# Layer 1's modulation vectors: from TensorE matmuls to multiply-accumulate on VectorE

## The chip, the cores and the metric

One core of a Trainium2 chip runs the whole program. The metric is the device time of one execution in microseconds (us), the median of several runs. A profiled execution gives the trace from which the rows below are taken. TensorE is PE in the profile (PEld are its weight loads), VectorE is DVE, ScalarE ACT, GpSimd POOL, and SP is the engine whose queue issues all loads.

## The reference

Two layers run over 256 context tokens and 256 latent tokens of 1024 channels, in fp32. At the head of each layer stand six modulation vectors per stream (shift, scale and gate for the mixer, and the same for the channel part):

```
sc, scc = silu(c), silu(c_ctx)                  # 1024 values each
mod_x = split(sc  @ mod_w[i] + mod_b[i], 6)     # mod_w[i]: 1024 x 6144
mod_c = split(scc @ mod_w[i] + mod_b[i], 6)
h  = rmsnorm(x) * (1 + scale) + shift;  x = x + gate * mixer(h)
h2 = rmsnorm(x) * (1 + scale2) + shift2;  x = x + gate2 * ffn(h2)
```

The context stream does the same with `mod_c`. Layer 0 has a dense feed-forward part (SwiGLU with 2816 hidden channels), layer 1 a top-2-of-8 mixture of experts. In the last layer the context is needed only for the recurrence's final state, so of `mod_c` only the first two vectors are used there. The modulation vectors depend on `c` and `c_ctx` alone, so layer 1's can be made at any time before its first norm.

## The kernel before

Tokens lie along the free dimension (context 0 to 255, latent 256 to 511), channels along the partitions in 8 tiles of 128. A projection goes *piece* by piece: a piece is 128 output channels x 1024 inputs of weights (128x1024 fp32, 512 KB). Each piece is split into a high and a low half by `split`/`hilo` (L160 on ACT makes `wh`, L161 on DVE makes `wl`; three buffers of each), and `mm` (L245 to L247) runs 8 x 3 matmuls of 512 columns for it (high x high, high x low, low x high) into one PSUM bank, then calls `tick`. DVE takes the pieces as they come; splits are put ahead in the order of issue by a priority.

The weights of the dense part come in chunks of four pieces (2 MB) into the `raw` ring of two buffers, all through SP's queue, in the order of the list `PLAN`, which `_stream_plan` writes at build time. `hold` hands out the pieces and fetches the next chunk when the last one is used up. A chunk `("mod", i, q)` in that list is not handed out: it starts `mod_chunk(i, q)`, which runs as a background generator stepped by `tick`.

`mod_chunk` makes four blocks of 128 modulation values for both streams from one 2 MB chunk. The weights are the moving operand: 8 matmuls (L341) of 512 columns, their stationary operand 32 columns wide, in four column groups of the array, add up in the PSUM tile `pmod`. For layer 1 four chunks share one bank; then ACT copies it to `ev` (L346), four small matmuls against `sel` add up the partial sums into `pmt` (L351), and one DVE addition (L365) puts them with the bias into `mod[1]`, a 128x48x2 tile (block, stream). Layer 1's twelve chunks stand in `PLAN` behind the first four chunks of layer 0's branch projections, and behind the chunks of `MOD_AFTER` in its feed-forward part.

`ffn` works in groups of 256 hidden channels, `NG` = 11. The first two groups run stream by stream on two held chunks. Then for each g from 2 to 10 `up(g)` runs four full-width pieces (two of w1, two of w3; Silu on ACT, product at L700 and its low half on DVE), and `down(g-2)` projects two pieces back: 8 x 2 x 3 matmuls (L719 to L721) and 16 residual updates on DVE (L554). At the end the last three groups are projected stream by stream, with layer 1's first norm (which reads `mod[1]`) as background work in between. Hidden tiles are four `ya` buffers a group, of sixteen; the tags `g` (16 buffers) and `cv` (8) are tiles of 128x512 which the mixer uses otherwise.

Everything is scheduled at build time: the order in time of each engine is a fixed list in which work that is not ready yields to work that is, and semaphores make each instruction wait for its data and buffers.

Of the kernel before, what the change touches and what calls it, by code (L numbers as in the profile page):

```python
# [6 lines left out]
F32 = mybir.dt.float32  # L7
F32R = mybir.dt.float32r
I32 = mybir.dt.int32
AF = mybir.ActivationFunctionType  # L10
# [75 lines left out]
def _chunks(p):  # L86
    return [p[q:q + 4] for q in range(0, len(p), 4)]
# [25 lines left out]
def _stream_plan():  # L113
    plan = [("lru", 0, 0), ("lru", 1, 0)]
    for n, c in enumerate(_chunks(_win_order(0))):
        if n == 0:
            plan += [("mod", 0, 0), tuple(c)] + [("mod", 0, q) for q in range(1, 4)]
        else:
            plan.append(tuple(c))
        if 2 <= n < 10:  # L120
            plan.append(("mod", 0, n + 2))
    for n, c in enumerate(_chunks(_branch_order(0))):
        plan.append(tuple(c))
        if n < 4:
            plan.append(("mod", 1, n))
    q = 4
    for n, c in enumerate(_chunks(_ffn_order() + _win_order(1) + _branch_order(1))):
        plan.append(tuple(c))
        if n in MOD_AFTER:
            plan.append(("mod", 1, q))  # L130
            q += 1
    assert q == 12, q
    return plan


NG = NF // 2
MOD_AFTER = (3, 5, 6, 8, 9, 11, 12, 14)
PLAN = _stream_plan()


class Trunk:
    def __init__(self, ctx, tc, wd, wm, xt, vec, out, dbg=None, stop=None):
        self.tc, self.nc = tc, tc.nc
        self.wd, self.wm, self.xt_d, self.vec_d, self.out = wd, wm, xt, vec, out
        self.dbg, self.stop = dbg or {}, stop
        self.ci = DEPTH
        self.ahead = 100
        self.last_act = None
        self.gate = None
        self.moddue = False  # L150
        self.pend = []
        self.bgs = []
        self.run(ctx)

    def v(self, key, i=0, n=1):
# [44 lines left out]
    def tick(self):  # L200
        for g in list(self.bgs):
            self.step(g)
        self.start_mod()

    def drain(self):
        while self.bgs:
            self.tick()

    def split(self, src):
        hi = self.hl.tile([P, PIECE], F32R, tag="wh", name="wh")  # L210
# [529 lines left out]
    def ffn(self, X, h, nxt):  # L740
        upn = lambda g: [self.hold((w, 0, 2 * g + f)) for w in ("w1", "w3") for f in range(2)]
        dnn = lambda g: [self.hold(("w2", 0, 2 * g + f)) for f in range(2)]
        hid = {}

        def new(g):
            hid[g] = [(self.t2("ya", "hh", F32R), self.t2("ya", "hl", F32R)) for f in range(2)]
            return hid[g]

        r0, r1 = upn(0), upn(1)
        new(0)  # L750
        new(1)
        for s in range(2):
            for g, r in ((0, r0), (1, r1)):
                self.up(r, h, s * TC, (s + 1) * TC, hid[g])
            if s == 0:
                self.drain()
        for g in range(2, NG):
            u = upn(g)
            self.up(u, h, 0, T, new(g))
            if g < NG - 1:  # L760
                self.down(dnn(g - 2), hid.pop(g - 2), X)
        self.drain()
        self.preload(AF.Sqrt)
        last = range(NG - 3, NG)
        r = [dnn(g) for g in last]
        for s in range(2):
            self.down_last(r, [hid[g] for g in last], s, X)
            nxt(s)
        self.dump("xf0", X)
# [11 lines left out]
    def run(self, ctx):  # L781
        tc, nc = self.tc, self.nc
        self.cst = ctx.enter_context(tc.tile_pool(name="cst", bufs=1))
        self.vec = self.cst.tile([P, NV], F32, tag="vec", name="vec")
        xs = self.cst.tile([P, KD, TC], F32, tag="xs", name="xs")
        self.small = ctx.enter_context(tc.tile_pool(name="small", bufs=2))
        self.mod = [self.cst.tile([P, 48, 2], F32, tag=f"mod{i}", name=f"mod{i}") for i in range(DEPTH)]
        self.sc = self.cst.tile([P, KD, SCW], F32, tag="sc", name="sc")
        nc.sync.dma_start(self.vec[:, 0:NV0], self.vec_d[:, 0:NV0])
        nc.sync.dma_start(self.sc, self.vec_d[:, NV:NV + KD * SCW].rearrange("p (k m) -> p k m", m=SCW))  # L790
        self.act_f(self.sc, self.sc, AF.Silu)
        W = dict(reuse_waits="tile")
        tags = {"ya": 16, "g": 16, "cv": 8, "hx": 16, "lt": 2}
        left, right, base = ExitStack(), ExitStack(), ExitStack()
        xc = left.enter_context(tc.tile_pool(name="xc", bufs=1)).tile([P, KD, TC], F32, tag="xc", name="xc")
        X = [(xc[:, k, :], xs[:, k, :]) for k in range(KD)]
        self.psum = base.enter_context(tc.tile_pool(name="psum", bufs=8, space=bass.MemoryType.PSUM))
        self.hl = left.enter_context(tc.tile_pool(name="hl", bufs=3))
        self.raw = left.enter_context(tc.tile_pool(name="raw", bufs=2))
        actr = right.enter_context(tc.tile_pool(name="actr", bufs=1, side="right"))  # L800
        self.lrup = right.enter_context(tc.tile_pool(name="lrup", bufs=2, side="right"))
        self.t2 = lambda tag, name, dt=F32: (actl if tag == "ya" else actr).tile(
            [P, 512], dt, tag=tag, name=name, bufs=tags[tag])
        start = tc.tile_pool(name="start", bufs=2)
        self.start = start.__enter__()
        m0 = self.chunk(("mod", 0, 0), self.start)
        for k in range(0, KD, 2):
            for s, t in enumerate((xc, xs)):
                nc.sync.dma_start(t[:, k:k + 2, :], self.xt_d[s, :, k:k + 2, :])
        hx = self.pairs("hx")  # L810
        self.lru_begin(0)
        u = self.begin(X, hx, m0)
        self.lru_consts()
        start.__exit__(None, None, None)
        actl = left.enter_context(tc.tile_pool(name="actl", bufs=1, **W))
        m = self.mixer(0, X, hx, u)
        self.preload(AF.Sqrt)
        h2 = self.pairs("hx")
        gs2 = self.gains(0, "n2", 4)

        def norm2(s, j):
            if j == 7:
                self.bgs.append(self.norm_steps(0, X, s * TC, (s + 1) * TC, gs2, 3, h2))

        self.mix_out(0, X, m, (0, 1), norm2)
        if self.stop == "m0":
            self.drain()
            left.close(), right.close(), base.close()
            return
        hx1 = []  # L830

        def norm1(s):
            if s == 0:
                hx1.extend(self.pairs("hx"))
            self.bgs.append(self.norm_steps(1, X, s * TC, (s + 1) * TC, self.gains(1, "n1", 1), 0, hx1, LAG1[s]))

        self.ffn(X, h2, norm1)
        self.lru_begin(1)
        m = self.mixer(1, X, hx1)
        self.preload(AF.Sqrt)  # L840
        right.close()
        self.mrawa = ctx.enter_context(tc.tile_pool(name="mrawa", bufs=RINGA, side="right", **W))
        self.rp = ctx.enter_context(tc.tile_pool(name="rp", bufs=1, side="right", **W))
        self.ptok = None
        self.bgs.append(self.route_begin())
        self.tick()
        self.mi, self.mq = 0, []

        def route(s, j):
            if j < 3:  # L850
                for _ in range(RINGA // 3):
                    self.mfetch()
            if j:
                self.route_tile(X, j - 1)

        self.mix_out(1, X, m, (1,), route)
        self.route_tile(X, KD - 1)
        assert self.ci == len(PLAN) and not self.bgs
        left.close()
        if self.stop == "m1":  # L860
            base.close()
            return
        self.mtok = ctx.enter_context(tc.tile_pool(name="mtok", bufs=1, **W))
        self.mrawb = ctx.enter_context(tc.tile_pool(name="mrawb", bufs=RINGB, **W))
        self.hl = ctx.enter_context(tc.tile_pool(name="mhl", bufs=3, **W))
        self.mp = ctx.enter_context(tc.tile_pool(name="mp", bufs=1, **W))
        self.moe(X)
        base.close()
# [452 lines left out]
def layout(inputs):  # L1321
# [51 lines left out]
    for n, what in enumerate(PLAN):  # L1373
        if what[0] == "mod":
            _, i, q = what
            w = a["mod_w"][i].reshape(KD, P, 48, P)
            cols = [2 * q, 2 * q + 1, KD + 2 * q, KD + 2 * q + 1] if i == 0 and q < 4 else range(4 * q, 4 * q + 4)
            d = wd[n].reshape(P, KD, 4, P)
# [21 lines left out]
        wm[:, :, 0:2].reshape(NE, NMC, 2, P, KD // 2, 2, 256)[:, :, :, :, :, g] = w  # L1400
    wm[:, :, 2] = a["moe_w2"][0].reshape(NE, NMC, 2, P, D).transpose(0, 1, 3, 2, 4).reshape(NE, NMC, P, MCH)
    wm = wm.reshape(NE * NJ, P, MCH)
    return {"wd": wd, "wm": wm, "xt": np.ascontiguousarray(xt), "vec": vec}


# [17 lines left out]
```

## Time and profile before

| | |
|---|---|
| median of 3 runs | 1915.62 us (1915.62 to 1917.23) |
| the profiled execution | 1915.24 us, span 1913.5 us |
| mean granted TensorE clock | 0.988 |
| busy, share of the span | PE 97%, PEld 74%, DVE 64%, ACT 47%, POOL 0% |
| HBM read | 445.73 MB |

The span runs from the first to the last instruction; what is outside it is start and end of the program. Busy time is the time in which at least one instruction of an engine is under way. Matmuls are pipelined, so the time between the starts of two of them says more than their durations.

### The profile page before, as it was taken

To read this page: it belongs to the slowest core of one execution; us is meant where nothing else is said; L and a number is where in the kernel's file an instruction comes from. 1 tells how busy PE (TensorE), PEld (TensorE's weight loads), DVE (VectorE), ACT (ScalarE), POOL (GpSimd) and SP (SyncE) were. 2 spreads that over 40 slices of the span, in tenths; PEclk is the share of its full clock that TensorE was granted. 3 is DMA by queue.
4 is the path that set the end of the run, shared out by engine and by line. 5 is a ranking of instruction groups with operands and counts; after the bars stand their busy time and mean duration, and the time that the engine had idled before them with its cause. 6 is when DMAs were issued, how large, how long until landed. Compare 5 with 4: busy or idle time off the path is not lost. (4 is left out here: it accounts for less than half of the span.)

```text
span 1913.5 us, 26733 instructions
## 1 busy us (share of the span) xinstructions
PE 1853.5 (97%) x10508; PEld 1420.8 (74%) x10508; DVE 1215.8 (64%) x1995; ACT 893.5 (47%) x1265; POOL 0.2 (0%) x4
## 2 busy tenths in 40 slices
PE   6999999999999999999999999899999999999997
PEld 3667777777997777779778899687578658767853
DVE  3899995355664544545899665786289249618932
ACT  4685322343552122134689464674167137416711
POOL 0000000000000000000000000000000000000000
PEclk8999999999999999999999999799999999999999
DMA  9234444244233244241233447689999999999994
GB/s 350 99 109 144 170 176 176 88 153 156 89 111 144 104 188 159 101 191 60 100 110 133 176 177 286 253 339 364 419 419 417 388 419 419 389 411 419 417 394 162
DMA packets 54277, 448.59 MB, mean 234 GB/s; under 512 B 6016, under 2 KB 7168, under 8 KB 10496
## 3 DMA queue, kind: packets, MB, share of 16 engines
q1 hardware_dynamic: 54144, 446.80, 59.8%
q8 instruction: 85, 1.39, 0.3%
q14 instruction: 48, 0.39, 0.1%
HBM read 445.73 MB, written 1.05 MB: 233 GB/s over the span
## 5 line engine op out<-in xcount | busy, mean ns | idle before, releaser
L160 ACT ACTIVATE wh<-raw 128x1024 fp32r<-128x1024 f32 (+1 forms) x237 | 246.9, 1053 | 455.1 <-PE ps L246 256.3
L161 DVE TENSOR_TENSOR wl<-raw,wh 128x1024 fp32r<-128x1024 f32 (+1 forms) x237 | 285.9, 1216 | 179.7 <-ACT wh L160 177.1
L161 DVE TENSOR_TENSOR wl<-mraw,wh 128x1024 fp32r<-128x1024 f32 x264 | 314.5, 1222 | 35.7 <-ACT wh L160 29.2
L160 ACT ACTIVATE wh<-mraw 128x1024 fp32r<-128x1024 f32 x264 | 272.8, 1058 | 51.5 <-PE s L1159 37.8
L245 PE MATMUL ps<-nh,wh 128*128 128x512 f32 (+1 forms) x736 | 274.1, 372 | 1.8 <-ACT wh L160 1.8
L247 PE MATMUL ps<-nh,wl 128*128 128x512 f32 (+1 forms) x736 | 269.5, 366 | 3.1 <-DVE wl L161 3.1
L246 PE MATMUL ps<-nl,wh 128*128 128x512 f32 (+1 forms) x736 | 269.3, 366 | 0.0
L245 PEld LDWEIGHTS ps<-nh,wh 128*128 128x128 f32 x736 | 139.5, 190 | 38.4 <-issue 4.7
L1170 PE MATMUL s<-mraw,xes 128*64 128x256 f32 x1408 | 162.0, 380 | 0.0
L247 PEld LDWEIGHTS ps<-nh,wl 128*128 128x128 f32 x736 | 139.5, 190 | 27.9 <-DVE wl L161 3.3
L246 PEld LDWEIGHTS ps<-nl,wh 128*128 128x128 f32 x736 | 139.5, 190 | 25.0 <-issue 1.4
L1160 PE MATMUL s<-wl,xe 128*128 128x512 f32 x352 | 140.5, 399 | 4.2 <-DVE wl L161 4.2
L1158 PE MATMUL s<-wh,xe 128*128 128x512 f32 x352 | 143.0, 406 | 0.0
L228 ACT ACTIVATE hd<-s 128x256 f32<-128x256 f32 (+1 forms) x88 | 28.9, 328 | 242.6 <-PE s L1170 218.6
L1159 PE MATMUL s<-wh,xe 128*128 128x512 f32 x352 | 139.0, 395 | 0.0
L1170 PEld LDWEIGHTS s<-mraw,xes 128*64 128x64 f32 x1408 | 98.4, 137 | 44.8 <-issue 0.7
L1179 DVE TENSOR_TENSOR hd<-hd,s 128x256 f32<-128x256 f32 (+1 forms) x88 | 30.9, 351 | 129.8 <-ACT hd L228 129.8
L544 DVE SCALAR_TENSOR_TENSOR cv<-v,vec,cv 128x254 f32<-128x254 f32 (+14 forms) x240 | 102.5, 469 | 0.8
L1160 PEld LDWEIGHTS s<-wl,xe 128*128 128x128 f32 x352 | 66.9, 190 | 23.0 <-DVE wl L161 8.9
L1225 PE MATMUL y<-mraw,hs 128*64 128x512 f32 x352 | 83.4, 595 | 0.4 <-DVE hs L1204 0.4
L1158 PEld LDWEIGHTS s<-wh,xe 128*128 128x128 f32 x352 | 67.3, 191 | 13.4 <-ACT wh L160 0.6
L1159 PEld LDWEIGHTS s<-wh,xe 128*128 128x128 f32 x352 | 67.2, 191 | 12.7
(278 smaller groups left out, 3474.0 us busy)
## 6 DMA issues: line engine op xcount, KB each, us to landing
mraw<-in_wm_dram SPq DMA_DIRECT2D x264, 1024.0 KB, 9.4
raw<-in_wd_dram SPq DMA_DIRECT2D x77, 2048.0 KB, 7.8
lw<-in_wd_dram SPq DMA_DIRECT2D x16, 256.0 KB, 2.7
xc<-in_xt_dram SPq DMA_DIRECT2D x4, 256.0 KB, 10.9
xs<-in_xt_dram SPq DMA_DIRECT2D x4, 256.0 KB, 10.8
out_dram<-xs SPq DMA_DIRECT2D x8, 128.0 KB, 2.0
vec<-in_vec_dram SPq DMA_DIRECT2D x1, 636.0 KB, 15.4
vec<-in_vec_dram SPq DMA_DIRECT2D x1, 317.0 KB, 2.9
```

The costliest lines, as they stand in the source:

```text
L160: return (self.nc.scalar.activation(hi, src, AF.Copy), self.nc.vector.tensor_tensor(lo, src, hi.bitcast(F32), op=ALU.subtract))
L161: self.nc.vector.tensor_tensor(lo, src, hi.bitcast(F32), op=ALU.subtract))
L245: self.nc.tensor.matmul(o, wh, ah, start=(k == 0), stop=False)
L246: self.nc.tensor.matmul(o, wh, al, start=False, stop=False)
L247: self.nc.tensor.matmul(o, wl, ah, start=False, stop=(k == KD - 1))
L544: nc.vector.scalar_tensor_tensor(cv[:, a0:a1], v[:, a0 + d:a1 + d], w(t), cv[:, a0:a1], op0=ALU.mult, op1=ALU.add)
L1158: nc.tensor.matmul(p1, xe[0][:, k, :], wh[:, cs], start=(k == 0), stop=False)
L1159: nc.tensor.matmul(p1, xe[1][:, k, :], wh[:, cs], start=False, stop=False)
L1160: nc.tensor.matmul(p1, xe[0][:, k, :], wl[:, cs], start=False, stop=(k == KD - 1))
L1170: nc.tensor.matmul(p1[r, 0:2 * P].rearrange("p (g f) -> p g f", g=2), xe[:, k, :], w[:, :, h * P:(h + 1) * P], start=(k == 0), stop=(k == ...
L1179: self.nc.vector.tensor_tensor(hd, hd, p1[:, n:2 * n], op=ALU.mult)
L1225: ins = self.nc.tensor.matmul(py[0][r, :], hs[:, f * HALF:(f + 1) * HALF], raw[:, f * PIECE + q * 512:f * PIECE + (q + 1) * 512], start=(c ...
```

## The change

Layer 1's twelve `mod` chunks leave `PLAN`. In their place a generator `mod_rows` runs in `ffn` from g = 2 on, one step with each `tick`, and `down` is followed by a `tick` more. That is six steps to a group. It loads `silu`'s arguments, `c` and `c_ctx`, each laid out as a row on all 128 partitions (`sr`, four tiles of 128x512 in `ya` buffers), and applies Silu on ACT. Then for each of the 48 blocks it has the weights with the 128 output channels on the partitions and the 1024 inputs along the free dimension (`wv`, two tiles of 128x512 in `cv` buffers, loaded two steps ahead). One DVE instruction per half multiplies the weights by the row and keeps the sum over its 512 columns (`accum_out`); blocks 0 to 15 do so for both streams, blocks 16 to 47 for the latent stream alone. A small instruction adds the two halves and the bias into `mod[1]`, which a memset on GpSimd has set to zero at the start. The products themselves go to a `g` tile that nobody reads.

```diff
@@ _stream_plan @@
         plan.append(tuple(c))
-        if n < 4:
-            plan.append(("mod", 1, n))
-    q = 4
-    for n, c in enumerate(_chunks(_ffn_order() + _win_order(1) + _branch_order(1))):
-        plan.append(tuple(c))
-        if n in MOD_AFTER:
-            plan.append(("mod", 1, q))
-            q += 1
-    assert q == 12, q
+    plan += [tuple(c) for c in _chunks(_ffn_order() + _win_order(1) + _branch_order(1))]
     return plan
...
@@ tick, drain @@
         self.start_mod()
+        if self.slow and next(self.slow, None) is None:
+            self.slow = None
 
     def drain(self):
+        slow, self.slow = self.slow, None
         while self.bgs:
             self.tick()
+        self.slow = slow
+
+    def mod_rows(self):
+        nc = self.nc
+        nb = 6 * KD
+        rows = [self.t2("ya", "scr") for _ in range(4)]
+        for q, t in enumerate(rows):
+            nc.sync.dma_start(t, self.sr[:, q * 512:(q + 1) * 512])
+            self.act_f(t, t, AF.Silu)
+        raw = {}
+
+        def fetch(b):
+            raw[b] = [self.t2("cv", "wv") for _ in range(2)]
+            for h, t in enumerate(raw[b]):
+                nc.sync.dma_start(t, self.wv[b, :, h * 512:(h + 1) * 512])
+
+        fetch(0)
+        fetch(1)
+        for b in range(nb):
+            yield 1
+            if b + 2 < nb:
+                fetch(b + 2)
+            n = 2 if b < 2 * KD else 1
+            acc = self.small.tile([P, 2, 2], F32, tag="acc", name="acc")
+            w = raw.pop(b)
+            junk = self.t2("g", "junk")
+            for s in range(n):
+                for h in range(2):
+                    nc.vector.scalar_tensor_tensor(junk, w[h], 1.0, rows[2 * s + h], op0=ALU.mult, op1=ALU.mult,
+                                                   accum_out=acc[:, h, s:s + 1])
+            nc.vector.scalar_tensor_tensor(self.mod[1][:, b, 0:n], acc[:, 0, 0:n], self.v(("mb", 1), b), acc[:, 1, 0:n],
+                                           op0=ALU.add, op1=ALU.add)
...
@@ ffn @@
+        self.slow = self.mod_rows()
         for g in range(2, NG):
             u = upn(g)
             self.up(u, h, 0, T, new(g))
             if g < NG - 1:
                 self.down(dnn(g - 2), hid.pop(g - 2), X)
+                self.tick()
+        while self.slow:
+            self.tick()
         self.drain()
...
@@ run @@
+        nc.gpsimd.memset(self.mod[1], 0.0)
...
@@ layout @@
+    wv = np.ascontiguousarray(a["mod_w"][1].T.reshape(6 * KD, P, D))
+    sr = np.tile(np.concatenate([a["c"][0], a["c_ctx"]])[None], (P, 1)).astype(f32)
```

## Rows read from the trace of the kernel before

**Rows 1.** The page's busy times: us, share of the span, number of instructions.

```profile
PE 1853.5 (97%) x10508; PEld 1420.8 (74%) x10508; DVE 1215.8 (64%) x1995; ACT 893.5 (47%) x1265; POOL 0.2 (0%) x4
```

**Rows 2.** Busy time by stage, as its header line names the columns.

```profile
core 0: us, PE busy (x) PEld busy (x) DVE busy (x) ACT busy (x) POOL busy (x), PEclk, DMA share, GB/s
391.00:470.80 79.80, 79.80 (x393) 60.28 (x392) 45.36 (x64) 33.52 (x44) 0.00 (x0) 1.00 0.47 169
565.00:868.00 303.00, 303.00 (x1376) 235.84 (x1375) 137.60 (x217) 74.25 (x90) 0.00 (x0) 1.00 0.38 146
1200.00:1913.00 713.00, 684.24 (x3976) 485.22 (x3976) 426.22 (x617) 342.08 (x475) 0.00 (x0) 0.98 0.93 376
```

**Rows 3.** PE's order of time, feed-forward stage: start, duration, line, tile, matmuls.

```profile
561.94 0.39 PE L245 MATMUL ps<-nh,wh 128*128 128x512 f32 x1
...
578.73 0.39 PE L245 MATMUL ps<-nh,wh 128*128 128x512 f32 x1
...
595.01 0.39 PE L721 MATMUL ps<-hh,wl 128*128 128x512 f32 x1
595.33 1.92 PE L341 MATMUL pmod<-raw,sc 128*32 128x512 f32 x16
597.18 0.50 PE L245 MATMUL ps<-nh,wh 128*128 128x512 f32 x1
597.52 0.39 PE L246 MATMUL ps<-nl,wh 128*128 128x512 f32 x1
```

**Rows 4.** The modulation matmuls' line: durations (ns), first and last start (us), forms.

```profile
L341 PE MATMUL pmod<-raw,sc x384: 592/592/1063, 12.1 to 850.7; 128*32 128x512 f32 x192
```

**Rows 5.** PE's order of time around one of the small sums.

```profile
714.34 0.40 PE L247 MATMUL ps<-nh,wl 128*128 128x512 f32 x1
...
715.38 0.48 PE L245 MATMUL ps<-nh,wh 128*128 128x512 f32 x1
715.70 0.39 PE L246 MATMUL ps<-nl,wh 128*128 128x512 f32 x1
```

**Rows 6.** DVE's order of time: start, duration, line, operation, tiles, [idle before].

```profile
54.96 0.17 DVE L365 TENSOR_TENSOR mod<-pmt,vec 128x8 f32<-128x8 f32 x1 [3.26 <-PE pmt L351]
55.16 0.16 DVE L370 SCALAR_TENSOR_TENSOR gs<-mod,vec 128x4 f32<-128x4 f32 x1
55.36 0.48 DVE L321 SCALAR_TENSOR_TENSOR nt<-xc,gs,prs 128x256 f32<-128x256 f32 x1
...
120.87 1.28 DVE L493 SCALAR_TENSOR_TENSOR gi<-gi,uc 128x512 f32<-128x512 f32 x2
122.07 0.54 DVE L537 TENSOR_SCALAR cv<-v,vec 128x512 f32<-128x512 f32 x1
...
631.20 2.35 DVE L161 TENSOR_TENSOR wl<-raw,wh 128x1024 fp32r<-128x1024 f32 x2
633.47 0.48 DVE L554 SCALAR_TENSOR_TENSOR xs<-ps,mod,xs 128x256 f32<-128x256 f32 x1
```

**Rows 7.** Order of time of ScalarE and DVE, splits in the feed-forward stage.

```profile
567.56 1.06 ACT L160 ACTIVATE wh<-raw 128x1024 fp32r<-128x1024 f32 x1 [4.11 <-PE ps L246]
...
568.65 1.23 DVE L161 TENSOR_TENSOR wl<-raw,wh 128x1024 fp32r<-128x1024 f32 x1 [3.91 <-ACT wh L160]
...
606.01 2.36 DVE L161 TENSOR_TENSOR wl<-raw,wh 128x1024 fp32r<-128x1024 f32 x2 [8.56 <-ACT wh L160]
```

**Rows 8.** Waits on SP and ScalarE, feed-forward stage: us in total, times, longest.

```profile
SPq L172 <- PE pmod L341: 130.5, 8, 26.8
...
ACT wh L160 <- DMA raw<-in_wd_dram: 9.0, 7, 1.5
```

**Rows 9.** The page's DMA issues: loads, KB of each, median us to landing.

```profile
raw<-in_wd_dram SPq DMA_DIRECT2D x77, 2048.0 KB, 7.8
lw<-in_wd_dram SPq DMA_DIRECT2D x16, 256.0 KB, 2.7
```

More of the change, by code (lines that the diff above doesn't have):

```diff
@@ L123, in _stream_plan, with __init__ @@
         plan.append(tuple(c))
-        if n < 4:
-            plan.append(("mod", 1, n))
-    q = 4
-    for n, c in enumerate(_chunks(_ffn_order() + _win_order(1) + _branch_order(1))):
-        plan.append(tuple(c))
-        if n in MOD_AFTER:
-            plan.append(("mod", 1, q))
-            q += 1
-    assert q == 12, q
+    plan += [tuple(c) for c in _chunks(_ffn_order() + _win_order(1) + _branch_order(1))]
     return plan
 NG = NF // 2
-MOD_AFTER = (3, 5, 6, 8, 9, 11, 12, 14)
 PLAN = _stream_plan()
 class Trunk:
-    def __init__(self, ctx, tc, wd, wm, xt, vec, out, dbg=None, stop=None):
+    def __init__(self, ctx, tc, wd, wm, wv, sr, xt, vec, out, dbg=None, stop=None):
         self.tc, self.nc = tc, tc.nc
+        self.wv, self.sr = wv, sr
         self.wd, self.wm, self.xt_d, self.vec_d, self.out = wd, wm, xt, vec, out
@@ L203, in tick @@
         self.start_mod()
+        if self.slow and next(self.slow, None) is None:
+            self.slow = None
     def drain(self):
+        slow, self.slow = self.slow, None
         while self.bgs:
             self.tick()
+        self.slow = slow
[27 more added lines that the diff above has]
+                                           op0=ALU.add, op1=ALU.add)
     def split(self, src):
@@ L1375, in layout @@
             _, i, q = what
+            assert i == 0
             w = a["mod_w"][i].reshape(KD, P, 48, P)
@@ L1402, in layout @@
     wm = wm.reshape(NE * NJ, P, MCH)
-    return {"wd": wd, "wm": wm, "xt": np.ascontiguousarray(xt), "vec": vec}
+    wv = np.ascontiguousarray(a["mod_w"][1].T.reshape(6 * KD, P, D))
+    sr = np.tile(np.concatenate([a["c"][0], a["c_ctx"]])[None], (P, 1)).astype(f32)
+    return {"wd": wd, "wm": wm, "wv": wv, "sr": sr, "xt": np.ascontiguousarray(xt), "vec": vec}
 def kernel(**inputs):
```

## The prediction

> **What bounds the kernel now.** First the page's busy times: TensorE (PE) is busy 97% of the span, VectorE (DVE) 64%, ScalarE 47% [rows 1]. That is an average, so next the table by stage [rows 2]. In the feed-forward stage of layer 0, from 565 to 868 us, PE is busy for all of the 303.00 us at a granted clock of 1.00 (2.4 GHz), DVE for 137.60, and the DMA engines for 0.38 of it. So this stage is as long as its matmuls, and DVE has 165 us to spare. The first four chunks, in the branch projections, find the same state: 79.80 of 79.80 us. In the expert stage from 1200 us PE is busy 684.24 of 713 us and DMA 0.93, but its loads begin with the second layer's output projection, so it only moves with what stands before it.
>
> Then the order in time on PE [rows 3]: a full-width piece, 24 matmuls, starts at 561.94 and the fourth of its group at 578.73, so a piece takes 5.60 us and matmuls follow each other every 0.233 us, with no gap. A group (four pieces up, then the 48 matmuls of the previous group's projection down) lasts from 561.94 to 595.24, one step after the last start at 595.01: 33.3 us.
>
> **What is removed.** Twelve chunks of modulation matmuls. For one, read the starts on both sides: the last matmul ahead starts at 595.01, the chunk runs, and the second matmul behind it starts at 597.52 [rows 3]. Two ordinary steps would have made that 595.47, so a chunk costs 2.05 us. All 192 modulation matmuls are on this one line, two records each [rows 4]; half of them, 96 in 12 chunks, are layer 1's. 12 x 2.05 = 24.6 us. After every fourth chunk, four small matmuls add up the partial results: from the last ordinary start at 714.34 to the second one behind at 715.70 are 1.36 us where 0.46 would do [rows 5], so 0.90 us, three times, 2.7 us. Together 27.3 us off an engine that waits for nothing there. ScalarE's three evictions of PSUM and DVE's three additions go too; both engines have room, so I count nothing.
>
> **What is added on DVE.** Per block of 128 channels two products with a running sum over 512 columns, for each of two streams in blocks 0 to 15 and for one in blocks 16 to 47: 16 x 4 + 32 x 2 = 128 such instructions, and 48 small ones that add the halves and the bias. The nearest instruction in the trace is the scalar-tensor-tensor that reads two 128x512 fp32 tiles in SBUF: two of them start at 120.87 and the next instruction at 122.07, so 0.60 us each [rows 6]. What the running sum adds, no row shows. The lower end is nothing; the upper end that I allow beside the rival below is one more of the smallest DVE instructions, whose starts lie 0.20 us apart (54.96, 55.16, 55.36) [rows 6]. A value per partition that has to be written out is nearest to that, so I take 0.80 us per instruction and 0.20 us for each small one. A block of two streams then takes 4 x 0.80 + 0.20 = 3.4 us, a block of one 1.8 us; in all 16 x 3.4 + 32 x 1.8 = 112 us (86 us at the lower end). (The Trainium skill, "VectorE: DVE Perf Modes", Two Vector instructions with no wait between them, says that an instruction that also writes out its accumulator is two instructions; no run here shows it yet, and it would put the price at the upper end.)
>
> Does this fit? Today's DVE work per group: the stage without its 8 chunks and two small sums is 303 - 18.2 = 284.8 us, 8.55 groups, so 137.6 / 8.55 = 16.1 us. One block goes with each of six steps per group. In the first 16 steps, 2.67 groups, DVE has to do 16.1 + 6 x 3.4 = 36.5 us while PE needs 33.3; it falls behind 3.2 us per group, 8.5 us in all. After that it has 16.1 + 6 x 1.8 = 26.9 us per 33.3 and catches up. How far may it be behind? Matmuls wait for the low half of the split weights, `wl`. The one that starts at 568.65, when the first piece of the group has given its buffer back, is done at 569.88 [rows 7], and with three buffers it belongs to the fourth piece, which starts at 578.73 [rows 3]: 8.8 us early. So the lag of 8.5 us just about fits in, and at 0.60 us per instruction (6 x 2.6 + 16.1 = 31.7) there is none. I count 2 us of PE waits, with ends of 0 and 8.5.
>
> **What moves on the load queue.** The chunks of 2 MB leave the ring of two `raw` buffers. Today loads on SP's queue waited 130.5 us for the modulation matmuls to give a buffer back [rows 8], and ScalarE waited for `raw` to land, 9.0 us in seven places [rows 8]; at one of them the split for the group's third piece began on DVE only at 606.01 and took 1.2 us [rows 7], with that piece due two pieces after 597.18, at 608.4. No matmul waited there, so losing these waits saves nothing but gives margin. New are 96 loads of 256 KB and four for the rows on the same queue. A 256 KB load lands in 2.7 us and a 2 MB chunk in 7.8 [rows 9]; DMA is 0.38 busy in the stage [rows 2], and about 9 MB more than today's 44 MB (303 us at 146 GB/s) keep it under 0.5. A block's load waits for the sums two steps before it, and a `raw` load behind it in the queue waits as well. The worst place is the chunk that a group needs first: it stands behind loads that wait for the sums of the step after the fourth piece. If DVE starts those as the piece starts, they end 3.4 us later, the chunk lands after 7.8 more, and the two halves of its first split (ScalarE's 1.06 [rows 7] and DVE's 1.14) end 13.4 us after the piece's start. The chunk's first matmul is due after 5.6 + 10.9 = 16.5. Margin about 3 us, so no wait is counted.
>
> The rest costs nothing: four Silu of 128x512 on ScalarE (busy 74.25 of the 303 us [rows 2]), four of sixteen `ya` buffers (three groups of hidden tiles, which is what a group needs, still fit into twelve), a memset on the idle GpSimd at the start, and results that are complete well ahead of the second layer's first norm.
>
> **Sum.** The profiled execution took 1915.24 us, 0.4 below the median of 1915.62. 1915.24 - 27.3 + 2 = 1889.9; I say 1890.
>
> **Rivals.**
> First, *the load queue*: DVE's lag of up to 8.5 us exceeds the margin of 3 us of the group's first chunk, so PE waits up to 5.5 us at one or two groups of the first three, and DVE, blocked behind a split whose data are late, loses time that it has not got. For it: the queue is in order. Against it: by the third group the lag shrinks. Price 5 to 15 us, about 1897, bounds 1893 to 1903.
>
> Second, *DVE becomes the bound*, the one on the other side: an instruction that reads two fp32 tiles and keeps a sum goes at half rate. Then 512 columns cost what 1024 cost now, 1.135 us each (two from 631.20, the next at 633.47 [rows 6]), plus 0.20, so 1.335. PE's wait is the lag less the lookahead: 64 p + 16 x 0.2 + 2.67 x 16.1 - 2.67 x 33.3 - 8.8, which is 64 p - 51.5 for a price of p. It begins at p = 0.80 and eats the whole gain at p = 1.23; at 1.335 it is 33.9 us, and a group of one-stream blocks (16.1 + 6 x 2.87 = 33.3) never catches up. 1915.24 - 27.3 + 33.9 = 1922; without the extra 0.20 (p = 1.135) it would be 1909. Against it: the plain form with the same two inputs runs at 0.60 us, 512 columns in half the time of 1024. For it: no row has a running sum. (The Trainium skill, "Vector Engine (DVE) Microarchitecture Reference", Points that are easy to get wrong, says just this: with two SBUF sources that aren't bf16 the throughput halves, because both read ports are taken. The trace of before speaks against it for the form without a sum; by the rule the time would be the 1909 to 1922 of this rival.)
>
> Third, *nothing is gained*, because something unseen paces the stage: 1915. PE without a gap speaks against it.
>
> **How the numbers follow.** Forecast 0.70 (1890; its own range 1886 to 1897, from the ends 0 and 8.5 us of wait); load queue 0.15; DVE at half rate 0.13, of which 0.09 lies above 1919.5, 0.02 within 0.2% and 0.02 below; nothing gained 0.02. About 0.2%, 3.8 us, is what a measurement of this kernel tells from no change. Faster 0.70 + 0.15 + 0.02 = 0.87, same 0.04, slower 0.09. The range goes from 1884 (some 4 us for PSUM and `raw` buffers that no longer hold anything up) to 1909 and leaves out a little over 0.1.
>
> **What would show it.** No modulation matmuls after 390 us; PE still busy all through the stage, now about 285 us from the same first piece; 128 instructions of 0.6 to 0.8 us each on DVE, and DVE full in the first three groups only. Wrong if those last over 1.2 us, if PE waits for `wl` or DVE's tiles in total more than some 10 us in the stage, or if ScalarE's waits for `raw` grow and matmuls wait behind them.

## The result and the profile after

The changed kernel takes 1891.78 us (median of 4 runs, 1890.26 to 1895.52) where the kernel before takes 1915.62 us beside it (4 runs, 1915.33 to 1917.23): a ratio of 0.9873, 95% interval 0.9860 to 0.9886, 24 us less. The forecast was 1890. The profiled execution is the slowest of the four, 1895.52 us with a span of 1893.6 us, against 1915.24 us before.

The page of the changed kernel: busy times (us, share of the span, number of instructions), the costliest new group of instructions, and the DMA issues that changed.

```profile
PE 1835.2 (97%) x10292; PEld 1421.2 (75%) x10292; DVE 1299.9 (69%) x2296; ACT 893.7 (47%) x1266; POOL 0.4 (0%) x5
...
L232 DVE SCALAR_TENSOR_TENSOR junk<-wv,scr 128x512 f32<-128x512 f32 x128 | 84.1, 687 | 0.2
...
raw<-in_wd_dram SPq DMA_DIRECT2D x65, 2048.0 KB, 7.4
wv<-in_wv_dram SPq DMA_DIRECT2D x96, 256.0 KB, 3.6
...
scr<-in_sr_dram SPq DMA_DIRECT2D x4, 256.0 KB, 4.9
```

PE has 216 instructions less than in [rows 1] and 18 us less busy time; DVE has 84 us more. The 128 sums were idle-free (0.2 us of idle time in all ahead of them), and the 2 MB loads land a little sooner than in [rows 9] although 100 loads have come between them.

The table by stage of the changed kernel: first the feed-forward stage between the same two points as in [rows 2] (19.3 us ahead of its first down projection, 1.0 us ahead of the last three groups), then its first five stretches of one group's length.

```profile
core 0: us, PE busy (x) PEld busy (x) DVE busy (x) ACT busy (x) POOL busy (x), PEclk, DMA share, GB/s
561.80:846.40 284.60, 284.60 (x1232) 230.98 (x1231) 219.16 (x513) 72.47 (x88) 0.00 (x0) 1.00 0.49 177
561.80:595.10 33.30, 33.30 (x146) 27.05 (x145) 30.19 (x76) 8.28 (x10) 0.00 (x0) 1.00 0.44 156
595.10:628.40 33.30, 33.30 (x146) 27.04 (x145) 31.79 (x81) 8.29 (x10) 0.00 (x0) 1.00 0.58 216
628.40:661.70 33.30, 33.30 (x146) 27.04 (x145) 31.08 (x81) 8.39 (x10) 0.00 (x0) 1.00 0.59 195
661.70:695.00 33.30, 33.30 (x146) 27.05 (x145) 24.79 (x58) 8.27 (x10) 0.00 (x0) 1.00 0.58 216
695.00:728.30 33.30, 33.30 (x146) 27.04 (x145) 24.71 (x57) 8.27 (x10) 0.00 (x0) 1.00 0.49 166
```

The stage lasts 284.6 us in place of 303.0, and PE is busy in all of it. DVE is nearly full in the first three stretches, into which the blocks with four sums fall, and has 8.5 us to spare from the fourth on. PE's order of time at the head of the stage, to be read beside [rows 3]:

```profile
558.70 0.40 PE L273 MATMUL ps<-nh,wh 128*128 128x512 f32 x1
558.93 0.39 PE L274 MATMUL ps<-nl,wh 128*128 128x512 f32 x1
...
591.76 0.39 PE L749 MATMUL ps<-hh,wl 128*128 128x512 f32 x1
591.99 0.40 PE L273 MATMUL ps<-nh,wh 128*128 128x512 f32 x1
```

The first group runs from 558.70 to 591.99, 33.29 us as before, and the next follows its last matmul by one step, 0.23 us, where the chunk stood. DVE's order of time at the first sums:

```profile
555.37 0.68 DVE L232 SCALAR_TENSOR_TENSOR junk<-wv,scr 128x512 f32<-128x512 f32 x1
555.98 0.08 DVE L232 DVE_READ_ACCUMULATOR junk<-wv,scr 128x1 f32 x1
555.98 0.69 DVE L232 SCALAR_TENSOR_TENSOR junk<-wv,scr 128x512 f32<-128x512 f32 x1
556.59 0.08 DVE L232 DVE_READ_ACCUMULATOR junk<-wv,scr 128x1 f32 x1
556.59 0.42 DVE L728 TENSOR_TENSOR s<-s,ps 128x256 f32<-128x256 f32 x1
...
562.64 0.23 DVE L234 SCALAR_TENSOR_TENSOR mod<-acc,vec 128x2 f32<-128x2 f32 x1
562.77 0.69 DVE L232 SCALAR_TENSOR_TENSOR junk<-wv,scr 128x512 f32<-128x512 f32 x1
```

From the start of a sum to the start of the instruction behind it are 0.61 us (555.37, 555.98, 556.59). Writing out its accumulator is an instruction of its own, of 0.08 us, but it starts together with the next instruction and costs no time of DVE's. The small instruction behind a block costs 0.13 us (562.64 to 562.77). The block isn't run in one go either: other products and splits go between its sums.

The waits of the feed-forward stage (545 to 870 us) in the changed kernel, total, times and longest, of ScalarE and PE, with the longest of SP's:

```profile
ACT wh L153 <- PE ps L274: 130.7, 35, 4.2
ACT wh L153 <- PE ps L748: 68.9, 8, 8.7
...
ACT wh L153 <- issue: 21.8, 6, 4.1
...
PEld pdn L747 <- issue: 0.8, 2, 0.4
...
PEld pdn L747 <- ACT wh L153: 0.4, 2, 0.2
...
SPq L218 <- DVE junk L232: 131.6, 62, 14.6
SPq L165 <- DVE wl L154: 97.2, 14, 21.7
```

The kernel before, waits of SP between the same two times:

```profile
SPq L172 <- DVE wl L161: 197.1, 11, 34.2
...
SPq L172 <- PE pmod L341: 55.7, 4, 14.2
```

So SP waits 131.6 us for sums where it waited 55.7 us for modulation matmuls. (The 130.5 us in [rows 8] are counted from 390 us on, so they hold the branches too.) All of SP's rows together are 256 us now and 338 us before. Nobody inherits the new wait: ScalarE waits for PE to give `wh` back, never for `raw` (9.0 us in [rows 8], no such row now), and PE itself has two rows, of 0.8 and 0.4 us.

### The profile page after: what moved, and what is told of

The parts are those of the page before. It is cut to its first block, busy times and chain, and to the rows that moved or that the text cites. A ratio compares the mean times of both kernels' runs of the same rounds, so it can differ in the third digit from the quotient of the medians.

```text
span 1893.6 us, 26822 instructions
## 1 busy us (share of the span) xinstructions
PE 1835.2 (97%) x10292; PEld 1421.2 (75%) x10292; DVE 1299.9 (69%) x2296; ACT 893.7 (47%) x1266; POOL 0.4 (0%) x5
## 5 line engine op out<-in xcount | busy, mean ns | idle before, releaser
L154 DVE TENSOR_TENSOR wl<-mraw,wh 128x1024 fp32r<-128x1024 f32 x264 | 314.6, 1222 | 35.8 <-ACT wh L153 29.2
L273 PEld LDWEIGHTS ps<-nh,wh 128*128 128x128 f32 x736 | 139.2, 189 | 31.1 <-ACT gab L256 1.7
L232 DVE SCALAR_TENSOR_TENSOR junk<-wv,scr 128x512 f32<-128x512 f32 x128 | 84.1, 687 | 0.2
L1191 PEld LDWEIGHTS s<-wh,xe 128*128 128x128 f32 x352 | 67.2, 191 | 13.4 <-ACT wh L153 0.7
```

Source lines behind the costliest of these rows:

```text
L154: self.nc.vector.tensor_tensor(lo, src, hi.bitcast(F32), op=ALU.subtract))
L232: nc.vector.scalar_tensor_tensor(junk, w[h], 1.0, rows[2 * s + h], op0=ALU.mult, op1=ALU.mult, accum_out=acc[:, h, s:s + 1])
L273: self.nc.tensor.matmul(o, wh, ah, start=(k == 0), stop=False)
L1191: nc.tensor.matmul(p1, xe[0][:, k, :], wh[:, cs], start=(k == 0), stop=False)
```

## The experiments

To see where time goes, all kernels are compared at the same five points of the order on PE: the first gate projection in layer 0's branches, the first matmul of the mixer's output projection, the first down projection, the first down projection of the last three groups, and the last combination of the experts. Start of the first point and the four lengths between them, in us, from the profiled execution of each. "Moved" is by how many bytes a partition the buffers of the split weights lie higher than in the kernel before.

| kernel | moved | first point | branches | output projection, two groups | feed-forward | rest | median |
|---|---|---|---|---|---|---|---|
| before | 0 | 102.6 | 364.4 | 117.3 | 284.7 | 1025.6 | 1915.62 |
| e1_no_sums | 0 | 101.8 | 356.3 | 116.5 | 266.4 | 1025.6 | 1888.63 |
| e8_after_acc_in_g | 0 | 102.5 | 356.3 | 116.5 | 266.4 | 1025.1 | 1889.04 |
| e5_before_pad64 | 64 | 103.8 | 365.4 | 119.2 | 284.4 | 1027.6 | 1921.02 |
| after | 64 | 105.5 | 357.3 | 118.3 | 266.3 | 1027.3 | 1891.78 |
| e3_sums_twice | 64 | 102.3 | 357.3 | 118.3 | 282.3 | 1029.2 | 1909.74 |
| e4_gate0_sums | 64 | 105.7 | 353.4 | 118.3 | 266.3 | 1027.5 | 1890.62 |
| e6_before_pad448 | 448 | 104.8 | 360.9 | 119.0 | 279.8 | 1027.7 | 1913.13 |
| e2_both | 448 | 101.9 | 360.9 | 119.0 | 279.7 | 1028.0 | 1911.84 |
| e7_after_pad384 | 448 | 104.4 | 352.7 | 118.1 | 261.1 | 1027.9 | 1882.45 |
| e9_gate0_pad384 | 448 | 103.4 | 348.5 | 118.1 | 261.1 | 1028.4 | 1880.47 |
| e10_after_pad448 | 512 | 103.7 | 356.3 | 116.5 | 266.4 | 1025.2 | 1890.73 |

**Without the sums.** The generator isn't started, so layer 1's vectors stay zero.

```diff
-        self.slow = self.mod_rows()
```

> The changed kernel with the generator of sums left out: no weight rows are loaded, nothing is added on VectorE, and layer 1's modulation vectors stay zero (its output is another one; the amount of work is the same). Theory (the sums are hidden behind the matmuls, the whole gain is TensorE's 27.3 us): 1915.6 - 27.3 = 1888, within 3 us of the changed kernel's 1891.8. Rival (the sums cost TensorE waits, so the gross gain is larger than what the changed kernel shows): 1885 or less, 7 us or more below the changed kernel.

Measured: 1888.63 us (4 runs, 1887.56 to 1890.22; ratio to before 0.9861, 0.9844 to 0.9877). The kernel before ran at 1916.12 us beside it, so 27.5 us are what the matmuls cost, as the first expectation had it. By the table: 8.1 in the branches, 0.8 in the next stretch (one small sum), 18.3 in the feed-forward part, 27.2 in all.

**Matmuls and sums.** The chunks go back into the list, and the sums are written to a tile that isn't read.

```diff
+        if n < 4:
+            plan.append(("mod", 1, n))
...
+        if n in MOD_AFTER:
+            plan.append(("mod", 1, q))
...
-            nc.vector.scalar_tensor_tensor(self.mod[1][:, b, 0:n], acc[:, 0, 0:n], self.v(("mb", 1), b), acc[:, 1, 0:n],
+            nc.vector.scalar_tensor_tensor(self.mod2[:, b, 0:n], acc[:, 0, 0:n], self.v(("mb", 1), b), acc[:, 1, 0:n],
...
+        self.mod2 = self.cst.tile([P, 48, 2], F32, tag="mod2", name="mod2")
```

> The changed kernel with layer 1's modulation matmuls put back where they stood; the sums are made as well, into a tile that nobody reads. Theory (only the matmuls have a price): 1915.6 to 1918, 24 us above the changed kernel. Rival (the loads of weight rows and of chunks hold each other up in the one queue once the chunks are in the ring again): 1920 to 1930, with waits of matmuls for split weights.

Measured: 1911.84 us (10 runs, 1909.62 to 1913.54; ratio 0.9978, 0.9969 to 0.9988). A kernel with all the work of before and all the sums besides is 4 us faster than before. So something else was gained, and by more than the sums can cost: by the table the feed-forward part is 5.0 us shorter and the branches 3.5, the two other lengths are 1.7 and 2.4 longer, with the same matmuls.

**Each sum twice.** DVE's added load is doubled.

```diff
-            for s in range(n):
+            for s in [q for q in range(n) for _ in range(2)]:
```

> The changed kernel with each sum instruction issued twice, so VectorE does 256 of them. Theory (VectorE falls behind within the first 2.67 groups and may be behind by 8.8 us only): at 0.61 us each a two-stream block takes 5.0 us, the lag is 64 x 1.22 + 16 x 0.13 + 43.0 - 88.9 = 34 us, 25 us of it beyond what the split buffers cover: 1917. Rival (sums may slip behind as long as nothing needs them, and only the stage's total counts): 137 + 256 x 0.61 + 6 = 299 us of VectorE work in a stage of 285 us, 15 us or less: 1900 to 1907. Third case (VectorE's load has no bearing): 1892.

Measured: 1909.74 us (6 runs, 1908.90 to 1912.92; ratio 0.9970, 0.9958 to 0.9983), 18 us above the changed kernel, between the two expectations. The feed-forward part is 16.0 us longer. The table by stage of this kernel, for the second, third and fourth stretch of one group's length:

```profile
591.90:625.20 33.30, 31.91 (x139) 25.66 (x138) 33.30 (x97) 8.48 (x10) 0.00 (x0) 1.00 0.50 185
625.20:658.50 33.30, 28.15 (x121) 22.19 (x119) 33.30 (x96) 4.73 (x5) 0.00 (x0) 1.00 0.40 136
658.50:691.80 33.30, 28.53 (x106) 22.10 (x107) 33.30 (x90) 7.05 (x8) 0.00 (x0) 0.85 0.41 140
```

and the longest of PE's waits in its feed-forward stage:

```profile
PEld ps L747 <- DVE s L728: 8.9, 2, 4.8
PE ps L747 <- DVE s L728: 8.0, 2, 4.4
PEld ps L275 <- DVE wl L154: 1.9, 1, 1.9
...
PE ps L273 <- DVE xs L582: 1.8, 2, 1.4
PE ps L275 <- DVE wl L154: 1.5, 1, 1.5
```

DVE is full in all three, and PE idles for 1.39 + 5.15 + 4.77 = 11.3 us. In the third of them, behind the stretch in which PE was busy for only 28.15 us, the granted clock is 0.85 on average, between its levels of 1.2 and 2.4 GHz: 106 matmuls in 28.53 us of busy time against 121 in 28.15, some 4 us more. So 11 us of waiting and 4 us of clock. PE's own rows are 8.0 us for the product of the hidden tiles (L728), 1.8 for a residual update and 1.5 for `wl`, the same 11.3 us. So the wait by which the prediction priced a lag, the one for `wl`, is the smallest. The prediction's formula gives 64 x 1.22 - 51.5 = 26.6 us for this load. It counts all of the lag beyond 8.8 us as waits; in the trace the last sum starts at 852.1 us, in the changed kernel at 807.8, so much of the backlog was left to later groups instead.

**The first layer's last two chunks by sums as well.** Blocks 40 to 47 of layer 0 (its feed-forward gate) leave the list too.

```diff
-        if 2 <= n < 10:
+        if 2 <= n < 8:
...
-        nb = 6 * KD
+        jobs = [(0, b) for b in range(5 * KD, 6 * KD)] + [(1, b) for b in range(6 * KD)]
+        nb = len(jobs)
...
-            n = 2 if b < 2 * KD else 1
+            i, k = jobs[b]
+            n = 2 if i == 0 or k < 2 * KD else 1
...
-        self.slow = self.mod_rows()
+                self.slow = self.mod_rows()
```

> The changed kernel, in which the last section of layer 0's modulation (blocks 40 to 47, the feed-forward gate) is made by sums as well: two more chunks of matmuls leave layer 0's mixer, eight more two-stream blocks (20 us of VectorE) are made in the feed-forward part, beginning with the second stream of its first two groups. Theory (a chunk costs 2.05 us wherever TensorE is full, VectorE has room in the feed-forward part): 4.1 us less than the changed kernel, 1887.7. Rival (VectorE is already full around the norm ahead of these steps, and splits of half-width pieces are needed every 2.8 us): no gain, 1892 to 1897.

Measured: 1890.62 us (4 runs, 1888.53 to 1892.91; ratio 0.9865, 0.9848 to 0.9881). The branches are 3.9 us shorter than after the change, for two chunks, 1.95 us each; the sums, 32 more, now begin at 537.4 us, and neither the stretch of the output projection nor the feed-forward part gets longer (118.3 and 266.3 us). The medians differ by only 1.2 us, between the two expectations and within the spread of the runs; they don't confirm the 3.9 us.

**Where the buffers lie.** By now one thing was left over: the changed kernel is 3 us slower than e1_no_sums although no matmul waits for a sum, e2_both is 4 us faster than before with more work, and the 256-column matmuls of the first two feed-forward groups have another pace from kernel to kernel. Their instructions are the same; their addresses aren't. The new tile `acc` and, in e2, `mod2` push all the buffers behind them on their side of the memory, those of the split weights among them, to higher addresses. Two kernels are before with an unused tile, one is after with such a tile, and one is after with `acc` in a `g` tile, so that nothing moves:

```diff
@@ e5_before_pad64; 112 in place of 16 in e6_before_pad448; on the changed kernel with 96 in e7_after_pad384 @@
+        nc.gpsimd.memset(self.cst.tile([P, 16], F32, tag="pad", name="pad"), 0.0)
@@ e8_after_acc_in_g @@
-            acc = self.small.tile([P, 2, 2], F32, tag="acc", name="acc")
+            acc = self.t2("g", "acc")[:, 0:4].rearrange("p (h s) -> p h s", s=2)
```

> The kernel before with a tile of 64 bytes per partition more among the constants, set to zero once; no other edit. It moves the buffers of the split weights to the addresses that they have in the changed kernel. Theory (the pace of the matmuls goes by where the split weights lie): half-width matmuls in the first two feed-forward groups every 0.1187 us as in the changed kernel instead of 0.1134, about 2 us more there, 1917 to 1919 in all if nothing else moves. Rival (the pace goes with the sums and their loads): 0.1134 and 1915.6 as before.

> The kernel before with a tile of 448 bytes per partition more, so the split weights lie where they lie in the run that made the vectors both ways. Theory (addresses): 1911 to 1912 as that run, with full-width matmuls of the feed-forward part at 0.2285 us on average instead of 0.2344 and half-width ones at 0.1200; then the sums of that run cost nothing. Rival (the extra sums or the extra step gained it): 1915.6.

> The changed kernel with a tile of 384 bytes per partition more; with its own 64 bytes for the sums the split weights then lie as in the run with both. Theory (addresses): its full-width matmuls run every 0.228 us or so in the feed-forward part, 4 to 5 us less than the changed kernel: 1886 to 1888. Rival (that run's pace came from its modulation chunks): 1891.8.

> The changed kernel with the sums' little tile taken from the buffers of 128x512 that the stage has anyway, so the split weights lie as in the kernel before. Theory (addresses, and the sums are hidden): half-width matmuls every 0.1134 us again, 2 us less than the changed kernel, within 2 us of the run without sums: 1888 to 1890. Rival (the sums slow the matmuls): 0.1187 and 1891.8.

Measured: e5_before_pad64 1921.02 us (9 runs, 1919.33 to 1923.22; ratio 1.0025, 1.0015 to 1.0035), e6_before_pad448 1913.13 (10 runs, 1909.58 to 1913.82; 0.9983, 0.9973 to 0.9992), e7_after_pad384 1882.45 (4 runs, 1881.05 to 1884.80; 0.9823, 0.9807 to 0.9840), e8_after_acc_in_g 1889.04 (4 runs, 1887.53 to 1889.30; 0.9861, 0.9844 to 0.9877). A tile that does nothing makes the old kernel 5 us slower or 3 us faster.

The pace can be read from the tables by stage, 15 us at the end of the first two groups, where all matmuls have 256 columns; the number in parentheses behind PE's busy time counts them. The kernel before (nothing moved):

```profile
529.30:544.30 15.00, 15.00 (x135) 15.00 (x134) 13.78 (x27) 12.55 (x22) 0.00 (x0) 1.00 0.01 2
```

The changed kernel (moved by 64 bytes):

```profile
526.10:541.10 15.00, 15.00 (x129) 15.00 (x128) 13.13 (x23) 11.19 (x21) 0.00 (x0) 1.00 0.01 2
```

e5_before_pad64 (64):

```profile
533.40:548.40 15.00, 15.00 (x128) 15.00 (x128) 13.13 (x23) 11.17 (x21) 0.00 (x0) 1.00 0.01 2
```

e7_after_pad384 (448):

```profile
520.20:535.20 15.00, 15.00 (x128) 15.00 (x126) 12.98 (x23) 11.43 (x21) 0.00 (x0) 1.00 0.01 2
```

e8_after_acc_in_g (0):

```profile
520.30:535.30 15.00, 15.00 (x135) 15.00 (x134) 13.78 (x27) 12.59 (x22) 0.00 (x0) 1.00 0.01 2
```

All run at a granted clock of 1.00 with PE never idle, and the count follows the address, not the change. The mean distance of starts there is 0.1133 us with nothing moved, 0.1187 with 64 bytes, 0.1200 with 448. Full-width steps go another way: in e7_after_pad384 they come every 0.2267 us, against 0.2333 in the changed kernel, as the order of time on PE shows with eight steps in 1.82 us in e7_after_pad384:

```profile
555.73 0.39 PE L274 MATMUL ps<-nl,wh 128*128 128x512 f32 x1
...
557.55 0.39 PE L273 MATMUL ps<-nh,wh 128*128 128x512 f32 x1
```

and in 1.87 us in the changed kernel:

```profile
574.33 0.39 PE L274 MATMUL ps<-nl,wh 128*128 128x512 f32 x1
...
576.20 0.39 PE L273 MATMUL ps<-nh,wh 128*128 128x512 f32 x1
```

The traces narrow it down. In these matmuls the activations (`nh`, `nl`) stay where they are in all twelve kernels: they lie in the pool `actr`, which is laid out from the other side of the memory (`side="right"`). In the down projection the activations (`hh`, `hl`) lie behind the added tiles and move together with the split weights, and there the pace stays. The kernel before, twelve steps in 2.72 us:

```profile
592.29 0.39 PE L721 MATMUL ps<-hh,wl 128*128 128x512 f32 x1
...
595.01 0.39 PE L721 MATMUL ps<-hh,wl 128*128 128x512 f32 x1
```

e7_after_pad384, twelve steps in 2.72 us:

```profile
583.16 0.39 PE L749 MATMUL ps<-hh,wl 128*128 128x512 f32 x1
...
585.88 0.39 PE L749 MATMUL ps<-hh,wl 128*128 128x512 f32 x1
```

Where PE doesn't wait, these steps are 0.2267 to 0.2274 us on average in all twelve kernels, and those of layer 0's output projection (256 columns, `mh` and `ml`, which move too) 0.1198 to 0.1199. So the pace doesn't go by the address of the weights alone; how weights and activations lie to each other fits all of these rows. Other tiles move with the weights as well, so it isn't shown that these two alone count.

e6_before_pad448 also settles e2_both: with the chunks alone, at the same place of the buffers, its four lengths are those of e2_both within 0.3 us, so the sums cost nothing there.

Now the change can be priced at one place of the buffers, by the sums of the three stretches that it touches: 364.4 + 117.3 + 284.7 to 356.3 + 116.5 + 266.4 with nothing moved, 27.2 us (e8); 27.1 us with 64 bytes (e5 to after); 27.8 us with 448 (e6 to e7). The medians of the same pairs differ by 27.2 (the kernel before ran at 1916.24 beside e8), 29.2 and 30.7 us; the 2 to 3 us that the last two have beyond their stretches stay open.

**Best of both, and 512 bytes.** The sums for layer 0's gate together with the better place, and the changed kernel moved by exactly 512 bytes.

```diff
@@ e9_gate0_pad384: on e4_gate0_sums; e10_after_pad448: on the changed kernel, 112 in place of 96 @@
+        nc.gpsimd.memset(self.cst.tile([P, 96], F32, tag="pad", name="pad"), 0.0)
```

> The changed kernel with layer 0's last two chunks of modulation by sums as well, and with a tile of 384 bytes a partition ahead of the weight buffers. If the two savings are independent, two chunks of 2.05 us less than the 1882.45 us of the padded kernel without the first: 1878.4 us, and the stretch from the second layer's pieces in the branch projections to the feed-forward stage is about 4 us shorter than the padded kernel's. The rival is that the first saving is mostly eaten by something in the program (its measurement alone gave 1.2 us): 1881 to 1882.5.

> The changed kernel with a tile of 448 bytes a partition, so that all the weight buffers lie 512 bytes above where they lie in the kernel before. If only the place within 512 bytes matters for the pace of matmuls, it runs as the changed kernel whose buffers lie where they did before: 1889 us, with half-width steps of 0.1134 us. If the place within 512 bytes doesn't decide, another pace: near the 1882 us of its neighbour 64 bytes below, with steps of 0.1200 us, or a value of its own.

Measured: e9_gate0_pad384 1880.47 us (5 runs, 1877.98 to 1881.34; ratio 0.9808, 0.9795 to 0.9821), the fastest version. Its branches are 4.2 us shorter than those of e7_after_pad384, as expected, its median is 2.0 lower, between the two expectations; the spread of the runs doesn't settle the rest. e10_after_pad448 1890.73 us (4 runs, 1888.61 to 1891.61; ratio 0.9869, 0.9854 to 0.9884). All four of its lengths are those of e8_after_acc_in_g within 0.1 us, and so is the pace in its table by stage:

```profile
521.50:536.50 15.00, 15.00 (x135) 15.00 (x134) 13.78 (x27) 12.55 (x22) 0.00 (x0) 1.00 0.01 2
```

So in this kernel a move by 512 bytes is like none, and the unused tile with its memset costs nothing by itself. A move by 448 bytes is worth 6.6 us (e8_after_acc_in_g to e7_after_pad384, 1889.04 to 1882.45, which ran beside each other).

## Why the prediction was right

**What was removed.** 12 x 2.05 + 3 x 0.90 = 27.3 us were counted; e1_no_sums measured 27.5, and the stretches give 8.1 for four chunks (counted 8.2), 0.8 for a small sum (0.9) and 18.3 for eight chunks and two small sums (18.2). Reading the starts on both sides of a chunk, instead of the matmuls' durations in [rows 4], gave the right price.

**What a sum costs on DVE.** Taken 0.80 us, measured 0.61, which is the lower end. The doubt was where the accumulator goes: it does go by an instruction of its own, as the Trainium skill says ("VectorE: DVE Perf Modes", Two Vector instructions with no wait between them), and the trace shows it with 0.08 us; but it runs beside the next instruction and adds nothing, so the upper end that I had tied to it didn't hold. The half rate of the rival with DVE as the bound (1.135 us) didn't come about: two fp32 tiles in SBUF and a running sum go at the pace of the form without a sum, 0.60 us in [rows 6]. On this the Trainium skill's "Vector Engine (DVE) Microarchitecture Reference", Points that are easy to get wrong, says that two SBUF sources that aren't bf16 halve the throughput; it differs from the trace, and the trace decides.

**Does it fit.** At the lower end, 0.60 us, a group of two-stream blocks was to take 31.7 us on DVE; the first three stretches show 30.2, 31.8 and 31.1 of 33.3. There was no lag, so the 2 us of PE waits were not there (their lower end, 0). That the room is real, and about how large, e3_sums_twice shows: at double the load DVE is the bound, the stage is 16.0 us longer, and the gain falls to 6 us. The formula with which the rival was priced would have said 26.6 us there, so it was too steep, and of the wait for `wl`, by which it counted, PE had only 1.5 us.

**The load queue.** No trace of the rival: SP waits 131.6 us for sums, but ScalarE no longer waits for `raw` in this stage. The margin of 3 us supposed that DVE starts a block's sums on time, and the lag of 8.5 us that was to use it up didn't arise. The 130.5 us that the prediction read as this stage's wait for modulation matmuls are 55.7 (the rest lies ahead of the stage); no term of the sum rests on it.

**The sum.** 1915.24 - 27.3 + 0 would have been 1887.9, and with the buffers left where they were it is 1889.04 (e8_after_acc_in_g), 0.4 us above the kernel without any sums (1888.63). The changed kernel stands 2.7 us higher, at 1891.78, because `acc` moves the weight buffers, and all others behind it, by 64 bytes; moving `acc` out of the way is all that e8_after_acc_in_g does, and the same move alone costs the kernel before 5 us (e5_before_pad64). The prediction had no such term. That it comes out within 2 us is luck: the 2 us of waits, which were not there, stood in for it. In the profiled execution the first point is also 2.9 us later than before; the changed kernel's other three runs are 2.7 to 5.3 us shorter than this one. No program was profiled twice, so whether this is only the run stays open.

## What to carry to other kernels

Where one engine is busy without a gap and another has room, price the work that is to move by the distance of starts on both sides of it, and check the room group by group, not over the span. When two builds differ by a few us, ask what else the edit moved: put a tile of the same size into the old kernel before anything is put down to the change itself. Here that was worth from 5 us more to 3 less, and up to 9 us less on the changed kernel.

## What the runs showed of the hardware

The pace of matmuls depends on where the data lie in SBUF, at a granted clock of 1.00 and with PE never idle: steps of 256 columns in the first two feed-forward groups take 0.1133, 0.1187 or 0.1200 us with the buffers moved by 0, 64 or 448 bytes, full-width steps of the up projections 0.2332 to 0.2333 us with 0 or 64 bytes, and 0.2267 with 448 (e7_after_pad384). With the chunks in between, the up projections' mean is 0.2344 and 0.2285 (the kernel before and e6_before_pad448), as the step behind a chunk takes 0.34 us. The best place for the one isn't the best for the other. 512 bytes give back the pace of 0, in the one kernel in which they were tried. Where the activations move together with the split weights, the pace is the same in all kernels (0.2267 to 0.2274 us in the down projections), so the weights' address alone doesn't decide. The place of the two to each other would fit, but other tiles move too, and no run told them apart; the mechanism stays open.
